# A hybrid decoder block on eight cores: interleaved query tiles, stationary P^T, resident MLP weights, and the normalisation of x from a host-transposed copy

## Chip, cores, metric

The kernel runs on all 8 NeuronCores of one Trainium2 chip. The metric is the device time of the slowest core in microseconds. A program on all cores has a fast state and a slow one, in which the cores of a die show a lower clock and take longer. The ratios below are of fast runs alone, and the profiles shown are of fast runs; a time in us given for a run is the median of all its executions.

Engine names in the profile: PE is the matrix engine (PEld its weight loads, which overlap it), ACT the activation engine, DVE the vector engine, POOL and SP the two that issue DMA (transfers between DRAM and on-chip memory) here. PSUM is the memory that PE writes its results to. The granted clock is the share of PE's full clock that the throttle let through. POOL issues the loads that cast fp32 to bf16, SP all others. L386 means line 386 of that kernel's source.

## The reference

Four sequences of 4096 tokens, width 1024. Cut to what matters:

```python
xn = rmsnorm(x, norm_mix_g)                      # per token
u = xn @ w_in                                    # 5120 columns: conv b,c,v | q,k,v | two gates
y_a = short_gated_conv(b_g, c_g, v_a, conv_w) @ w_a_out
s = q k^T / 8 - slope_h * (i - j), causal        # 4 heads, two softmax maps each
o = (softmax(s0) - lam * softmax(s1)) @ v        # then rmsnorm over the head's 128 values
x = x + (g_a * y_a + g_b * (o @ w_b_out)) @ w_o
x = x + relu(rmsnorm(x) @ w_mlp_in)**2 @ w_mlp_out
return rmsnorm(x) * norm_final_g
```

Two cores share a sequence. Each computes K and V for all 4096 tokens and the rest for 2048 queries of its own.

## The kernel before

Every engine has its own in-order instruction list; a recorder turns buffer reads and writes into semaphores. The parts that matter (cuts marked `# ...`):

```python
# phase 1: a token tile is squared, scaled, and transposed by PE
S.op("act", ... activation(xb, xt, AF.Square, accum_out=st[:, 0:1]) ...)
S.op("act", ... Ln ...); S.op("act", ... Exp, scale=-0.5 ...)        # rstd, per partition = per token
S.op("dve", ... tensor_scalar_mul(xb, xt, st[:, 2:3]) ...)
for c in range(8):
    S.op("pe", ... transpose(pst[:, c, :], xb[:, c*128:(c+1)*128], ident) ...)
S.op("dve", ... tensor_tensor(dst, pst, gcols, ALU.mult) ...)        # x normalised and transposed
# ...
# phase 2: a step = 128 keys x 512 queries x 2 maps
def emit_pv(n):        # V stationary, P^T moving
    mm(Ops[:, m, cs:512], Vt[:, kt, h*128:(h+1)*128], PT[:, m, cs:512], ...)
def emit_lsum(n):      # row sums: ones stationary, P^T moving
    mm(Lps[:, m, cs:512], ones_bf, PT[:, m, cs:512], ...)
# per head: copy O and L, 128x1024 reciprocal, multiply, subtract, norm
# ...
S.barrier()            # between projections, attention, gates, MLP
# phase 4: eight groups of 512 hidden columns, W1 and W2 streamed, x_mid accumulated by DVE
```

The softmax here doesn't subtract the row's maximum and nothing guards it: scores larger than these inputs give would overflow.

## Time and profile before

| run | us |
|---|---|
| fast runs of the first four | 1544.24, 1546.27 |
| slow runs of the first four | 1663.52, 1740.64 |

The page of the profiled run gives busy time per engine, and PE's busy share and granted clock in 40 equal slices (9 is 90% or more):

```profile
span 1546.6 us, 22141 instructions; the slowest of 8 cores (1531.8 to 1546.6 us)
...
PE 1376.5 (89%) x6824; PEld 584.5 (38%) x6824; DVE 709.2 (46%) x963; ACT 712.6 (46%) x1066; POOL 67.5 (4%) x72
...
PE   1989999878999999999367888897999999999995
...
PEclk9999999989999999999788999999999999999998
```

PE is nearly full apart from the first slice, the change from attention to gates (slices 20 and 21) and the gates, where it is busy 255 of 321 us. The table by windows says the same by stage. Its columns are: window and length, busy us of each engine with instructions in brackets, granted clock, DMA share, GB/s. The rows are projections, attention, gates and merge, MLP, last norms.

```profile
0.00:291.00 291.00, 244.32 (x1352) 118.44 (x1352) 134.20 (x231) 94.97 (x210) 5.29 (x13) 0.99 0.37 84
291.00:760.00 469.00, 431.35 (x2176) 149.91 (x2176) 197.45 (x111) 347.48 (x350) 2.38 (x3) 0.96 0.06 10
760.00:1081.00 321.00, 255.22 (x1250) 115.91 (x1248) 136.91 (x213) 160.16 (x306) 29.73 (x34) 0.91 0.54 86
1081.00:1507.00 426.00, 425.38 (x1959) 192.30 (x1960) 214.07 (x364) 81.24 (x140) 11.32 (x14) 0.99 0.22 36
1507.00:1546.60 39.60, 20.28 (x91) 7.90 (x88) 26.56 (x45) 28.70 (x60) 18.78 (x8) 0.84 0.53 212
```

One step of attention in the timeline (start, length, engine, what):

```profile
601.13 1.04 PE L348 MATMUL ps_all<-big 128*128 128x512 bf16 x4
601.30 1.11 ACT L675 ACTIVATE big<-ps_all,big 128x1024 bf16<-128x1024 f32 x1 [0.18 <-PE ps_all L350]
602.10 0.39 PE L350 MATMUL ps_all<-big 64*128 64x512 bf16 x2
602.42 1.04 PE L348 MATMUL ps_all<-big 128*128 128x512 bf16 x4
```

From one group of four to the next it is 602.42 - 601.13 = 1.29 us, of which the exponential takes 1.11. PE binds, and ACT is close.

### The profile page before, as it was taken

The numbers are of one execution on the slowest core, as the hardware profiler recorded it, in microseconds if no ns is written. First come the engines' busy times: TensorE is split into PE (matmuls) and PEld (weight loads), VectorE is DVE, ScalarE is ACT, GpSimd is POOL, SyncE is SP. The second block draws the span as 40 slices with busy tenths as digits, with TensorE's granted clock in tenths as the row PEclk, the third lists the DMA queues.
The fourth block names the chain that finished last, engine by engine and source line by source line (L and its number), as shares of the span: only waits on it lengthen the run. The fifth ranks groups of instructions, "written<-read, shape, count | busy, mean of one in ns | idle before, by whom it ended". The sixth has DMA issues, their size and how long they took to land.

```text
span 1546.6 us, 22141 instructions; the slowest of 8 cores (1531.8 to 1546.6 us)
## 1 busy us (share of the span) xinstructions
PE 1376.5 (89%) x6824; PEld 584.5 (38%) x6824; DVE 709.2 (46%) x963; ACT 712.6 (46%) x1066; POOL 67.5 (4%) x72
## 2 busy tenths in 40 slices
PE   1989999878999999999367888897999999999995
PEld 0444444323333333333123434343444444444441
DVE  2444454476553332333323454455253563564476
ACT  2553322356778878888244555463312112102217
POOL 0000000000000000000000000000000000000004
PEclk9999999989999999999788999999999999999998
DMA  8861100330000000000197254443331313121105
GB/s 163 182 159 53 44 28 1 54 56 1 1 1 1 1 1 1 1 0 1 19 259 103 36 74 53 57 56 55 53 57 31 53 29 55 28 32 25 28 11 208
DMA packets 63907, 80.06 MB, mean 52 GB/s; under 512 B 2984, under 2 KB 48168, under 8 KB 63792
## 3 DMA queue, kind: packets, MB, share of 16 engines
q0 software_dynamic: 53120, 44.04, 20.2%
q1 hardware_dynamic: 10672, 34.60, 7.0%
q8 instruction: 58, 0.95, 0.2%
q14 instruction: 57, 0.47, 0.1%
HBM read 114.29 MB, written 8.39 MB: 79 GB/s over the span
## 4 chain that ended last, share of the span: by engine, by line
PE 77%; DVE 8%; DMA 5%; ACT 5%; issue 3%; SPq 0%; POOL 0%; POOLq 0%; DVEq 0%; ACTq 0%
PE ps_all L348 70%; PE ps_all L350 6%; DMA big<-w_in 3%; DMA big<-xs 2%; DVE big L706 2%; DVE big L700 1%; DVE big L809 1%; ACT big L675 1%; ACT big L962 1%; ACT big L790 1%; PE ps_all L387 1%; PE ps_all L807 1%; ACT big L973 1%; DVE big L856 0%; DVE big L390 0%
## 5 line engine op out<-in xcount | busy, mean ns | idle before, releaser
L348 PE MATMUL ps_all<-big 128*128 128x512 bf16 (+3 forms) x5600 | 1270.6, 378 | 98.9 <-ACT big L834 24.4
L348 PEld LDWEIGHTS ps_all<-big 128*128 128x128 bf16 x5600 | 517.4, 100 | 741.2 <-issue 212.1
L675 ACT ACTIVATE big<-ps_all,big 128x1024 bf16<-128x1024 f32 (+1 forms) x320 | 329.1, 1049 | 101.2 <-PE ps_all L350 68.0
L997 ACT ACTIVATE big<-ps_all 128x512 bf16<-128x512 f32 x128 | 76.4, 597 | 319.1 <-PE ps_all L348 319.1
L1011 DVE TENSOR_TENSOR big<-ps_all,big 128x512 f32<-128x512 f32 x256 | 175.7, 690 | 39.3 <-PE ps_all L348 36.1
L350 PE MATMUL ps_all<-big 64*128 64x512 bf16 (+3 forms) x736 | 130.0, 350 | 11.6 <-ACT big L675 6.9
L998 DVE TENSOR_TENSOR big<-big 128x512 bf16<-128x512 bf16 x128 | 54.4, 425 | 175.9 <-ACT big L997 175.9
L706 DVE RECIPROCAL big<-big 128x1024 f32<-128x1024 f32 x16 | 104.8, 6552 | 2.0 <-DVE big L705 0.5
L700 DVE COPY big<-ps_all 128x1024 f32<-128x1024 f32 x16 | 19.6, 1222 | 175.5 <-PE ps_all L348 175.5
L350 PEld LDWEIGHTS ps_all<-big 64*128 64x128 bf16 x736 | 36.1, 93 | 147.6 <-issue 141.3
L850 DVE TENSOR_TENSOR big<-ps_all,big 128x512 f32<-128x512 f32 x32 | 22.1, 691 | 143.7 <-PE ps_all L348 94.1
L790 ACT ACTIVATE big<-big 128x1024 bf16<-128x1024 f32 x28 | 29.6, 1056 | 96.9 <-DVE big L789 91.3
L366 ACT ACTIVATE big<-big 128x1024 bf16<-128x1024 f32 (+1 forms) x33 | 34.9, 1058 | 56.9 <-DVE big L488 26.2
L319 POOL DMA_DIRECT2D big<-w_in x34 | 29.9, 883 | 710.3 <-DVE big L725 469.3
L387 PE MATMUL ps_all<-big 128*128 128x128 bf16 (+1 forms) x264 | 21.5, 228 | 39.4 <-DVE big L365 31.0
L376 DVE TENSOR_SCALAR big<-big 128x1024 bf16<-128x1024 f32 (+1 forms) x33 | 25.0, 759 | 53.1 <-ACT big L370 53.1
L390 DVE TENSOR_TENSOR big<-ps_all,big 128x1024 bf16<-128x1024 bf16 (+1 forms) x33 | 39.1, 1186 | 3.4 <-PE ps_all L387 3.3
L705 DVE COPY big<-ps_all 128x1024 f32<-128x1024 f32 x16 | 19.6, 1224 | 41.5 <-PE ps_all L348 41.4
L401 DVE CAST big<-ps_all 128x512 bf16<-128x512 f32 x24 | 16.5, 688 | 43.0 <-PE ps_all L348 43.0
L387 PEld LDWEIGHTS ps_all<-big 128*128 128x128 bf16 (+1 forms) x264 | 18.2, 102 | 47.1 <-issue 40.9
L725 DVE SCALAR_TENSOR_TENSOR big<-big 128x512 bf16<-128x512 f32 x16 | 12.0, 750 | 50.5 <-ACT big L724 50.5
L834 ACT ACTIVATE big<-ps_all,big 128x512 f32<-128x512 f32 x32 | 21.7, 679 | 27.3 <-PE ps_all L348 27.3
(67 smaller groups left out, 558.9 us busy)
## 6 DMA issues: line engine op xcount, KB each, us to landing
big<-xs SPq DMA_DIRECT2D x48, 512.0 KB, 7.8
big<-w_in POOLq DMA_DIRECT2D x32, 512.0 KB, 6.8
big<-w POOLq DMA_DIRECT2D x16, 1024.0 KB, 8.7
out<-big SPq DMA_DIRECT2D x16, 512.0 KB, 2.9
big<-w_in POOLq DMA_DIRECT2D x4, 1024.0 KB, 33.3
big<-w_in POOLq DMA_DIRECT2D x1, 2048.0 KB, 25.0
big<-w_o POOLq DMA_DIRECT2D x1, 2048.0 KB, 29.0
big<-w_a POOLq DMA_DIRECT2D x1, 1024.0 KB, 12.1
```

The lines of the kernel that those rows point to most:

```text
L348: S.op("pe", lambda e: e.matmul(out, lhsT, rhs, start=start, stop=stop), reads=reads, writes=writes)
L350: S.op("pe", lambda e: e.matmul(out, lhsT, rhs, start=start, stop=stop, tile_position=tp), reads=reads, writes=writes)
L366: S.op("act", lambda e: e.activation(xb[:ntok], xt[:ntok], AF.Square, accum_out=st[:ntok, 0:1]), reads=[xkey, skey], writes=[xbkey, skey])
L387: S.op("pe", lambda e, c=c: e.transpose(pst[:, c, :ntok], xb[:ntok, c * 128:(c + 1) * 128], ident[:ntok, :ntok]), reads=[xbkey, "ident"], ...
L390: S.op("dve", lambda e: e.tensor_tensor(dst, pst[:, :, :ntok], gcols.unsqueeze(2).to_broadcast([128, 8, ntok]), ALU.mult), reads=[pkey, gk ...
L675: S.op("act", lambda e: e.activation(PT[:, :, cs:512], Sps[:, buf, :, cs:512], AF.Exp, bias=btab[:, bidx:bidx + 1], scale=0.125), reads=[" ...
L700: S.op("dve", lambda e: e.tensor_copy(c["Ocp"], Ops), reads=["O"], writes=[c["k"] + "O"])
L706: S.op("dve", lambda e: e.reciprocal(c["Lcp"], c["Lcp"]), reads=[k + "L"], writes=[k + "L"])
L790: S.op("act", lambda e: e.activation(xb, xt, AF.Square, accum_out=st[:, 0:1]), reads=[xkey, skey], writes=[xbkey, skey])
L997: S.op("act", lambda e, r=r, ph=ph: e.activation(r, ph, AF.Relu), reads=[phk], writes=[rk])
L998: S.op("dve", lambda e, r=r, fc=fc, sl=sl: e.tensor_tensor(hb[:, fc, sl * 512:(sl + 1) * 512], r, r, ALU.mult), reads=[rk], writes=["h2_%d ...
L1011: S.op("dve", lambda e, T=T, half=half, pz=pz: e.tensor_tensor(x_mid[:, T, half * 512:(half + 1) * 512], pz, x_mid[:, T, half * 512:(half ...
```

## The change

The intent: halve PE's work for PV by making P^T the stationary operand, with V and a column of ones moving, so the row sum comes along; give each core every second 128-query tile, so that causal trimming acts on both halves of the keys; have the host hand over x transposed, so that PE transposes no norms; keep MLP weights resident and accumulate over all 4096 hidden columns in PSUM; remove barriers. The source has a mode that interleaves projections with attention; in this version it is off. A rewrite, so only its core is shown (cuts marked `...`):

```diff
-    mm(Ops[:, m, cs:512], Vt[:, kt, h*128:(h+1)*128], PT[:, m, cs:512], ...)
-    mm(Lps[:, m, cs:512], ones_bf, PT[:, m, cs:512], ...)
+    mm(oview(m, t), PT.ap[:, m, t*128:(t+1)*128], v.ap[:, h, 0:129], start, ..., skip=True)
...
-    # Square, Ln, Exp, scale, 8 PE transposes, multiply by g       (per 128 tokens)
+    def xT_load(blk, pieces=2):                    # x^T from the host, cast by POOL's DMA
+        wload(XT[s], xT_d[blk], q * n, n, 512)
+    def load_tok(blk, t):                          # the same tokens again, for the statistics
+        ld(xt.ap, xs_d[r0:r0 + 128, :], [xt])      # two buffers, SP
+    def row_bcast(blk, src, dst, n, p):            # rstd: one per partition -> one per column
+        row = rr_sp[blk, 0:n]                      # a DRAM scratch row
+        S.dma("sp", ... dma_start(out=row.rearrange("(t p) -> p t", p=128), in_=src.ap[:, 0:4]))
+        ld(dst.ap, rr_sp[blk:blk+1, 0:n].partition_broadcast(128), [dst], [key])
+    def nrm(c):                                    # x^T * g * R, by DVE, 8 of them
+    steps = [a, sq(0), sq(1), sq(2), sq(3), r, b, nrm(0), nrm(2), nrm(4), nrm(6)]   # + spill of xn
...
+    W += spread(conv(1) + kv(6), prelude(2))       # a block's prelude runs in the block before it
+    plan = PLAN if merge else [(n_a0, 0), (n_a1, 0), (n_a2, 0), (n_a3, 0)]          # merge=False
...
+    m_w1()                                         # W1 (8 x 2 MB fp32) and a quarter of W2: POOL
+    until(10 ** 9 if False else sum(1 for k, _ in W if k))    # last conv, gates, merge
+    for q in (1, 2, 3): cload(W2[q]...)
+    m_load(0)                                      # MLP input back from its spill: SP
```

Block 4, the first, needs no row: its rstd is applied to the exponent's scale and to V, where it is per partition.

## The prediction

> Times are fast-state (before: 1544 us; I take its runs of 1664 and 1741 for slow).
>
> **What bounds it now.** Page: PE busy 1376 of 1547 us; chain of waits 77% PE. By windows:
> - 0-281 us, projections: first matmul group at 38 us, then PE nearly full.
> - 295-760, attention: a full step (128 keys x 512 queries x 2 maps) takes 1.29 us (timeline): four 128x512 matmuls 0.86, the QK pair with array-mode switches 0.43. The exponential takes 1.11, so PE binds, ACT close behind. The first four heads take 17 us each behind a DVE chain with a 6.55 us reciprocal.
> - 760-1081, gates: PE busy 254 of 321; idle for weight DMA (767-820) and the norm chain (Square, scale, transpose, L809).
> - 1081-1507, MLP: PE 100%, 215 ns per matmul.
> - 1507-1547: final norms.
>
> **Unchanged:** about 4096 dense matmuls x 215 ns = 882 us.
>
> **What the change does.**
> 1. PV and row sums: P^T stationary, V plus a ones column moving; the build has 2176 matmuls of 129 columns for 1280 mostly 512 wide. Warm 128-wide transposes cost 56 ns each here (16 in 1.06 us, 8 in 0.61): 122 us for about 260. The Trainium skill ("TensorE: Matmul & The Clock Gate", Back-to-back issue gap) gives 81 ns sustained at N=128; this trace shows 56.
> 2. Attention becomes ACT-bound. 384 exponentials (168 of 1024, 152 of 512, 24 of 768, 40 of 256) at before's 1.11/0.69/0.90/0.48 us = 332 us, like before's 329: finer trimming is spent on splitting head 0 in two. Back to back, ACT instructions overlap by 0.09 us: 300 to 332. Add group 0 (DVE epilogue about 9 us per head), small pairs, and 6 us PE idle per flush: 360 to 390 against 465. PE idles 30% of it; nothing is interleaved.
> 3. Host-supplied x^T and folded scales remove norm transposes and stalls; reloads of spilled tiles return about 5 us per gate group, transposes 2 us.
> 4. The POOL queue is in order: W1 and a quarter of W2 (20 MB fp32) go ahead of the last gate weights and Wo (6 MB). Cast loads took 20.2% of 16 engines' span for 44 MB bf16: about 285 GB/s of fp32 (estimate). So Wo lands 90 us after attention 3, where PE could start z at 62: stall about 30 us. The conv weights queue behind attention 0's last POOL op: 13 us stall. At the start 14 MB precede the second K/V block: attention 0 starts near 73 us.
> 5. MLP 442 us plus 5-8 for reloading its input; tail 10 us for 39.
>
> **Sum.** Start 73; attention 45+70+105+139; projections between 69+57+57; last conv 21; gates 4x57+36+28 = 292; MLP 450; tail 10: about 1390. I say 1400, range 1335 to 1505 (high end: slow runs in a median). Faster 0.93, same 0.04, slower 0.03.
>
> **Right if** ACT is over 85% busy in attention groups 2 and 3, about 2.1 us per full pair; PV costs 56-60 ns; PE has a 15-35 us gap in gate group 0 ended by a w_g or w_o DMA; MLP matmuls stay at 215 ns; the tail is under 15 us.
>
> **Wrong if** PV costs 80 ns or more (+40 us); cast loads run below 250 GB/s (start and gate group 0, +30); flush and small-pair bubbles are twice mine; or denser matmuls draw a lower granted clock. Faster if large contiguous weight rows load well above 300 GB/s.

## The result

1799.18 us median of four (1785.01 to 1846.02); the two fast runs are 1799.94 and 1785.01. A ratio here is the mean time of one kernel's fast runs over that of the other's in the same rounds, so it isn't quite the ratio of the medians quoted. It is 1.1595, with a 95% interval of 1.1511 to 1.1679: the changed kernel is 16% slower.

The page after, the lines that answer to those above:

```profile
span 1798.4 us, 20663 instructions; the slowest of 8 cores (1776.2 to 1798.4 us)
...
PE 1267.2 (70%) x7168; PEld 611.5 (34%) x7168; DVE 501.3 (28%) x1135; ACT 529.0 (29%) x744; POOL 61.6 (3%) x97
...
PE   4055528266555759667772788797709999999998
...
PEclk9576669687777888677986678898959999999999
```

PE is busy 109 us less and idle for 531 us. The holes are in the first half. In the clock row, 9s appear mostly where PE is full. This trace holds two reduced clocks: 0.50 for 532 us of the core shown, against 120 us on the core shown of the kernel before, and 0.81 for 236 us between 682 and 1096 us. The 0.81 is seen on the four cores of die 0 only (104 to 243 us); die 1 has none and took 1781 us (median of its cores) against 1794, so it is worth some 13 us (an estimate from that difference). The windows below run from the first to the last exponential of each attention group, so odd rows are projections and even rows attention; then come last conv, gates and merge in one row, MLP, tail.

```profile
0.00:136.00 136.00, 44.91 (x162) 16.98 (x162) 23.67 (x49) 15.16 (x26) 12.75 (x25) 0.75 0.59 107
136.00:188.00 52.00, 29.93 (x230) 18.66 (x230) 29.71 (x109) 25.59 (x36) 3.02 (x3) 0.62 0.02 6
188.00:344.00 156.00, 67.31 (x335) 29.13 (x334) 43.64 (x92) 17.40 (x35) 8.53 (x13) 0.70 0.43 78
344.00:427.00 83.00, 54.91 (x547) 35.52 (x546) 28.88 (x107) 59.77 (x74) 3.02 (x3) 0.84 0.02 6
427.00:545.00 118.00, 64.38 (x271) 26.93 (x270) 39.45 (x81) 14.77 (x28) 5.25 (x7) 0.74 0.37 73
545.00:665.00 120.00, 84.18 (x870) 54.75 (x868) 31.04 (x111) 95.02 (x114) 3.02 (x3) 0.86 0.01 4
665.00:762.00 97.00, 72.51 (x268) 28.63 (x267) 38.59 (x78) 8.77 (x17) 5.46 (x9) 0.74 0.36 77
762.00:918.00 156.00, 116.44 (x1188) 75.24 (x1188) 26.93 (x104) 131.07 (x156) 3.42 (x4) 0.84 0.12 23
918.00:1346.00 428.00, 288.64 (x1259) 124.87 (x1256) 139.23 (x218) 66.95 (x105) 8.43 (x15) 0.79 0.50 120
1346.00:1790.00 444.00, 443.50 (x2047) 200.75 (x2048) 97.92 (x189) 93.33 (x158) 8.15 (x15) 1.00 0.13 46
1790.00:1798.40 8.40, 0.51 (x3) 0.01 (x1) 2.19 (x3) 1.15 (x2) 0.54 (x1) 0.74 0.15 62
```

| stretch | predicted | measured |
|---|---|---|
| projections, the four | 73+69+57+57 = 256 | 136+156+118+97 = 507 |
| attention, the four | 359 | 52+83+120+156 = 411 |
| last conv, gates, merge | 21+292 = 313 | 428, entry of the MLP included |
| MLP and tail | 460 | 452 |

The projections hold 251 us of the error. One of them, 427 to 545 us, in the chain of waits (start, length, what it stood on):

```profile
467.17 19.31 DMA rr_sp<-big
486.55 5.94 DMA big<-rr_sp
...
501.55 8.02 DMA big<-xs
...
512.18 4.37 DMA big<-xs
...
519.38 16.29 DMA rr_sp<-big
535.74 6.28 DMA big<-rr_sp
```

Twice in this stretch a row of 512 rstd values is written to DRAM (19.31 and 16.29 us) and read back over 128 partitions (5.94 and 6.28); the tokens for the second block's statistics are loaded only after the first block is normalised. PE is busy 64 us of the 118. The write also keeps the list of SP waiting: over the whole kernel SP stood 110.1 us, in eight waits, until such a write had landed, before it could issue the read and the loads behind it. The list of DMA issues (count, KB each, median us to landing) has both transfers:

```profile
rr_sp<-big SPq DMA_DIRECT2D x7, 2.0 KB, 16.3
big<-rr_sp SPq DMA_DIRECT2D x7, 256.0 KB, 6.3
```

Attention itself went as meant. A pair of key tiles in its steady part:

```profile
859.85 6.24 ACT L670 ACTIVATE big<-ps_all,big 128x1024 bf16<-128x1024 f32 x6
860.10 1.73 PE L386 MATMUL ps_all<-big 64*128 64x512 bf16 x20 [0.37 <-ACT big L670]
860.42 1.11 PEld L386 LDWEIGHTS ps_all<-big 128*128 128x128 bf16 x18 [0.23 <-issue]
862.11 1.73 PE L386 MATMUL ps_all<-big 64*128 64x512 bf16 x20 [0.29 <-ACT big L670]
```

A pair (two steps of the kernel before, 2.58 us there) takes 2.01 to 2.1 us (2.19 where the clock is 0.81), ACT runs without a gap, six exponentials in 6.24 us, and PE is idle 0.3 to 0.4 us of each pair. The Trainium skill ("ScalarE: Activation LUTs", What ACT_TABLE_LOAD costs) says that back-to-back ACTIVATEs overlap by about 93 ns; here six that take 1.11 us each alone (in the kernel before) take 6.24 in a row, 84 ns less at each of the five joints, which nearly agrees.

At the change from one head to the next it looks different (the second line is the window 850 to 855 us, columns as above):

```profile
849.33 4.84 PE L386 MATMUL ps_all<-big 128*128 128x129 bf16 x36 [3.63 <-DVE big L706]
850.00:855.00 5.00, 4.68 (x37) 3.20 (x36) 2.27 (x13) 2.21 (x2) 1.01 (x1) 0.50 0.02 5
```

PE waits 3.63 us, and then 36 matmuls take 4.84 us at a clock of 0.50, where 40 take 3.46 in the steady part. In the four attention stretches ACT is busy 311 of 411 us: it stands still 100 us, 6.2 us for each of the sixteen heads.

Two long PE waits follow later, at the first gate group and at the MLP (idle time before the group and its releaser in brackets):

```profile
981.00 3.57 PE L386 MATMUL ps_all<-big 128*128 128x512 bf16 x8 [27.55 <-DMA big<-xn_sp]
1001.86 56.21 PE L386 MATMUL ps_all<-big 128*128 128x512 bf16 x208 [17.29 <-DMA big<-ya_sp]
...
1346.50 3.93 PE L386 MATMUL ps_all<-big 128*128 128x512 bf16 x9 [47.61 <-DMA big<-x_sp]
```

### The profile page after: what moved, and what is told of

Its sections match the earlier page's. It is cut to its first block, busy times and chain, and to the rows that moved or that the text cites. A ratio compares the mean times of both kernels' runs of the same rounds, so it can differ in the third digit from the quotient of the medians.

```text
span 1798.4 us, 20663 instructions; the slowest of 8 cores (1776.2 to 1798.4 us)
## 1 busy us (share of the span) xinstructions
PE 1267.2 (70%) x7168; PEld 611.5 (34%) x7168; DVE 501.3 (28%) x1135; ACT 529.0 (29%) x744; POOL 61.6 (3%) x97
## 4 chain that ended last, share of the span: by engine, by line
PE 52%; DMA 24%; DVE 10%; ACT 7%; issue 4%; POOL 1%; DVEq 0%; SPq 0%; ACTq 0%; POOLq 0%
PE ps_all L386 51%; DMA big<-xs 7%; ACT big L670 6%; DMA rr_sp<-big 6%; DMA big<-ya_sp 3%; DMA big<-rr_sp 3%; DMA big<-x_sp 2%; DVE big L489 1%; DMA x_sp<-big 1%; DVE big L706 1%; DVE big L710 1%; DVE big L720 1%; POOL big L715 1%; ACT big L430 1%; DMA xm_sp<-big 1%
## 5 line engine op out<-in xcount | busy, mean ns | idle before, releaser
L386 PEld LDWEIGHTS ps_all<-big 128*128 128x128 bf16 (+1 forms) x6976 | 598.5, 103 | 1103.6 <-issue 700.4
L670 ACT ACTIVATE big<-ps_all,big 128x1024 bf16<-128x1024 f32 (+3 forms) x384 | 315.5, 882 | 240.1 <-PE ps_all L386 226.0
L780 ACT ACTIVATE big<-ps_all,big 128x512 f32<-128x512 f32 x64 | 44.0, 687 | 209.5 <-PE ps_all L386 209.5
L791 DVE SCALAR_TENSOR_TENSOR big<-big,ps_all 128x512 f32<-128x512 f32 x64 | 44.0, 688 | 178.3 <-PE ps_all L386 178.3
L489 DVE SCALAR_TENSOR_TENSOR big<-big 128x512 bf16<-128x512 bf16 x56 | 39.1, 744 | 166.6 <-DMA big<-rr_sp 166.6
L430 ACT ACTIVATE big<-big 128x1024 bf16<-128x1024 f32 x32 | 33.9, 1058 | 172.4 <-DMA big<-xs 172.0
L675 DVE TENSOR_TENSOR big<-big 128x256 bf16<-128x256 bf16 x64 | 18.7, 292 | 223.5 <-ACT big L670 223.5
L915 ACT ACTIVATE big<-big 128x1024 bf16<-128x1024 f32 x16 | 16.9, 1056 | 208.3 <-DVE big L910 208.3
L910 DVE SCALAR_TENSOR_TENSOR big<-ps_all,big 128x512 f32<-128x512 f32 x32 | 24.0, 751 | 163.2 <-PE ps_all L386 163.2
L818 ACT ACTIVATE big<-big 128x1024 bf16<-128x1024 f32 x16 | 16.9, 1057 | 74.0 <-DVE big L814 74.0
L727 PE MATMUL ps_all<-big 128*128 128x128 bf16 x64 | 8.1, 268 | 42.0 <-DVE big L720 42.0
L814 DVE SCALAR_TENSOR_TENSOR big<-ps_all,big 128x512 f32<-128x512 f32 x32 | 22.0, 689 | 34.9 <-PE ps_all L386 21.0
L828 PE MATMUL ps_all<-big 128*128 128x128 bf16 x128 | 11.5, 242 | 22.4 <-DVE big L817 22.3
L830 DVE TENSOR_TENSOR big<-ps_all,big 128x1024 bf16<-128x1024 bf16 x16 | 19.6, 1224 | 22.4 <-DMA x_sp<-big 20.7
```

Source lines behind the costliest of these rows:

```text
L386: S.op("pe", lambda e: e.matmul(out, lhsT, rhs, start=start, stop=stop, skip_group_check=skip), reads, writes)
L430: act(lambda e: e.activation(junk.ap, xt.ap, AF.Square, accum_out=ss1[blk].ap[:, t:t + 1]), [xt], [junk, ss1[blk]])
L489: dve(lambda e, k=k: e.scalar_tensor_tensor(x[k].ap, x[k].ap, ccol(C_GMIX + k), R_b.ap, ALU.mult, ALU.mult), [x[k], cst, R_b], [x[k]])
L670: act(lambda e, a=a, b=b, c=c, s=s, PT=PT, scale=scale: e.activation(PT.ap[:, :, a:b], Sb[s][:, :, a:b], AF.Exp, bias=ccol(C_BTAB + c), sc ...
L780: act(lambda e: e.activation(t.ap, ps, AF.Tanh, bias=hbg.ap[:, 8 * w + dm:8 * w + dm + 1], scale=0.5), [key, hbg], [t])
L791: dve(lambda e: e.scalar_tensor_tensor(t.ap, t.ap, 1.0, ps, ALU.add, ALU.mult), [key, t], [t])
```

## The experiments

Sixteen runs, three rounds each (five for the last); the kernel before had medians of 1544.2, 1547.42, 1548.49 and 1550.47 us. Gains in us are taken from the 1799 above. It includes two slow runs; the two fast ones are 15 us apart with a mean of 1792.5, and by fast runs alone most gains are some 5 to 8 us smaller. Theory A: the DRAM round trip of the rstd row, on a serial chain per block, holds the projections. Rivals: the denser matmuls draw a lower clock (B); the bytes of x, which are read twice (C); the separate stretches themselves; the in-order POOL queue.

### 1. No round trip, wrong values (e1_copy)

```diff
-        S.dma("sp", w, [src], [key])
-        ld(dst.ap, rr_sp[...].partition_broadcast(128), [dst], [key])
+        dve(lambda e: e.tensor_copy(dst.ap[:, 0:n], src.ap[:, 0:1].to_broadcast([128, n])), [src], [dst])
```

> The DRAM round trip of the rstd row is replaced by an on-chip copy with the same dependency (wrong values on purpose; same input bytes, same statistics). In the changed kernel the row write took 8 to 20 us to land and the broadcast read 5 to 16, seven times in series. Theory A (the round trip sits on a serial chain that bounds the projection stretches): the four stretches 0-146, 195-340, 437-572, 672-800 us (554 together, 330 to 360 of it idle or cold PE) fall to about 350 in sum, total 1560 to 1620, and the mean granted clock rises from 0.84 to 0.90 or more. Theory B (the denser matmuls draw a lower clock): the clock stays near 0.84, total within 3% of 1799. Theory C (the stretches are bound by the bytes of x, read twice): bytes are the same, so the total moves under 3%.

1614.2 us, 1.0445 of before (1.0421 to 1.0468), relative error 0.041 as intended. The four projection stretches:

```profile
0.00:84.00 84.00, 43.25 (x162) 16.64 (x162) 23.96 (x51) 15.16 (x26) 12.84 (x25) 0.86 0.77 166
137.00:234.00 97.00, 64.64 (x330) 28.48 (x328) 40.23 (x88) 15.63 (x31) 8.53 (x13) 0.84 0.54 119
320.00:390.00 70.00, 60.34 (x275) 26.55 (x273) 39.12 (x82) 13.86 (x26) 5.25 (x7) 0.93 0.49 115
511.00:580.00 69.00, 58.31 (x268) 25.84 (x266) 38.75 (x79) 8.97 (x17) 5.53 (x9) 0.93 0.43 97
```

They sum to 320 us in place of 507 (the expectation's 554 had wider edges), a gain of 187 us, which is the gain of the whole kernel (1799 - 1614 = 185; 178 by fast runs). The input bytes are the same, so C falls as the main cause. The mean granted clock went from 0.84 to 0.89 (0.90 was expected) and in these stretches from 0.70-0.75 to 0.84-0.93 without any matmul being changed, so most of the low clock followed from the idle PE; B falls as the main cause. The 0.81 on die 0 is absent from this run's trace, so it adds some 13 us to the comparison at most. The Trainium skill ("TensorE: Matmul & The Clock Gate", Part 1) describes a clock that rises with activity and falls back when PE idles, which agrees: 0.50 was granted for 351 to 371 us of each core here, and for 524 to 563 us in the changed kernel.

### 2. The same row in 16-byte runs, right values (e2_rows)

```diff
-        r0 = blk * 512 + t * 128
-        ld(xt.ap, xs_d[r0:r0 + 128, :], [xt])
+        rows = xs_d[blk * 512:(blk + 1) * 512, :].rearrange("(p t) d -> p t d", t=4)
+        ld(xt.ap, rows[:, t, :], [xt])
...
-        out=row.rearrange("(t p) -> p t", p=128)
+        out=row.rearrange("(p t) -> p t", t=4)
```

> Right values; the statistics tile holds tokens 4p+t, so the row is written as 128 runs of 16 bytes in place of 512 runs of 4 bytes. If the number of tiny writes makes the write slow, its landing falls from a median of 16 us to 5 or less and the total by about 60 to 90 us. If it is queueing behind the large loads or the receipt of a DRAM write, it stays over 10 us and the total within 2%.

1695.05 us, correct, 1.0928 of before (1.0903 to 1.0953): 104 us gained, more than the 60 to 90 expected, by choosing which tokens share a partition. The list of DMA issues:

```profile
rr_sp<-big SPq DMA_DIRECT2D x7, 2.0 KB, 2.5
big<-rr_sp SPq DMA_DIRECT2D x7, 256.0 KB, 4.4
```

The write fell from 16.3 to 2.5 us with the same 2 KB and the same loads around it, so it was the 512 runs of 4 bytes, not the writing to DRAM as such, that made it slow. The Trainium skill ("DMA: Bandwidth & Descriptors", Rules for kernel authors) says that a last dimension that isn't contiguous becomes one descriptor per element. This agrees: from the changed kernel (first line) to this run (second) the packets fall by 2688, which is 7 x (512 - 128).

```profile
DMA packets 38021, 119.57 MB, mean 66 GB/s; under 512 B 7680, under 2 KB 12160, under 8 KB 34464
DMA packets 35333, 119.57 MB, mean 71 GB/s; under 512 B 4992, under 2 KB 9472, under 8 KB 31776
```

The number of runs isn't all: the row for the convolution's halo (the tokens just before each query tile, 32 values) still goes as 4-byte runs in this kernel, and took 10.4 us in a stretch (186 to 200 us) in which the DMA engines were full.

### 3. Statistics one block earlier, round trip kept (e3_ahead)

```diff
-    R_b = ar.take("R", [512], F32)
+    R_r = [ar.take("R%d" % k, [512], F32) for k in range(3)]
...
-    W += spread(kvq(0), prelude(5))
+    W += spread(kvq(0), prelude(5, 1) + prelude_halo())     # normalise 5, statistics of 1
```

> Right values; the round trip is kept, but each block's statistics start one block earlier, with three row buffers, and the halo moves before attention 0. Theory A with the chain only exposed by lack of lookahead: PE waits for the normalised tiles shrink to under 100 us in sum, total 1560 to 1650, while the write still takes 10 us or more to land. If the loads of x (token-major) through two buffers and the in-order SP queue bind instead, the chain just shifts and the total falls by less than 60 us.

1711.02 us, correct, 1.1072 (1.1054 to 1.1091): 88 us gained, less than the 150 or more that was expected. The stretches became 163, 92, 88 and 68 us: the last three shrank by 123 us, and the start grew by 27, because two blocks' statistics now stand ahead of the first attention. The write still took 14.4 us. So in the later stretches much of the chain was exposed for want of lookahead; at the start there is nothing to hide it under.

### 4. Order of the weight bursts (e5_loads)

```diff
-    m_w1()
-    until(all chunks)
+    until(n_w1)          # after 16 chunks of gate group 0
+    m_w1()
+    until(n_g2 + 32)
+    m_load(0)            # MLP input back, during gate group 2
+    until(all chunks)
```

> Only DMA order in the gate and MLP stretches changes: the 20 MB burst of W1 and W2 starts after the 16th chunk of gate group 0, and the first MLP input tile is loaded back during gate group 2. Theory: the reload of the spilled tiles was starved by weight bursts on the same 16 DMA engines; then the 43 us gap at 959-1002 falls to 8 to 12, the 30 us gap ahead of the MLP to under 5, total 1730 to 1745 (3 to 4% less). Rival: the gaps are the latency of spill and reload itself; then they stay over 25 us each. Projections and attention are unchanged.

1738.71 us, correct, 1.1266 (1.1234 to 1.1298): 60 us less, in the expected range, but only in part for the expected reason. PE's waits at gate group 0 and ahead of the MLP (us in total, times, longest):

```profile
PE ps_all L386 <- DMA big<-xn_sp: 31.1, 1, 31.1
PE ps_all L386 <- DVE big L837: 3.5, 1, 3.5
```

The wait ahead of the MLP fell from 47.6 to 3.5 us. The waits in gate group 0 stayed (31.1 and 12.1 us against 27.6 and 17.3), because later in the program isn't later in time: POOL has nothing to wait for and runs ahead, and issued the burst at 934.28 us, before SP issued the reload at 937.94. By fast runs alone the gain is 53 us: 44 from the MLP's entry, and 8 from a projection start that was earlier in this run, which the edit doesn't explain.

### 5. Merged stretches, round trip kept (e4_merge)

```diff
-def build_program(merge=False):
+def build_program(merge=True):
```

> Right values; only the argument merge is turned on: the projections of the next group (and conv, gates after group 3) are issued between attention pairs by the kernel's own plan, everything else as changed, round trip included. If the separate stretches are the loss (theory: PE idles in attention about 40%, and the norm chain only runs outside it), the chain and its DRAM round trip hide under attention: total 1350 to 1500. Rival: the in-order queues carry the waits of the norm chain into attention (the Square on ACT and the row write on SP stand in the same queues as the exponentials and stores), so most of it stays exposed: total 1600 or more.

1744.81 us, correct, 1.1283 (1.1253 to 1.1313). Letting projections run between attention pairs is worth 54 us, not 300: the rival holds. The row writes are 8% of this run's chain of waits; the chain's Squares and DMA issues stand in the same in-order queues as the exponentials and the stores of attention. That its waits are carried along in them is a reading of the program, not shown; what the list of waits shows is that ACT still stood 137.6 us for the token loads ahead of the Squares (172.0 in the changed kernel).

### 6. Broadcast on PE, right values (e7_pebcast), and together with the loads (x_sep)

```diff
-        S.dma("sp", w, [src], [key])
-        ld(dst.ap, rr_sp[...].partition_broadcast(128), [dst], [key])
+        for t in range((n + 127) // 128):      # diagonal of rstd
+            dve(... tensor_scalar_mul(dgb.ap[:p, t*m:(t+1)*m], ident[:p, 0:m], src.ap[:p, t:t+1]) ...)
+        mm(ps[:, 0:n], ones_f.ap[:p, :], dgb.ap[:p, 0:n], True, True, ...)     # fp32
+        dve(... tensor_copy(dst.ap[:, 0:n], ps[:, 0:n]) ...)
```

> Right values; the row is broadcast on chip: diagonal of rstd times a matrix of ones in fp32 on PE (one 128x512 fp32 matmul per block, 0.63 us in the kernel before), no DRAM round trip. Theory A, as confirmed by the wrong-valued copy (1614): 1605 to 1650. If the copy was fast only because its values were degenerate or the halo was taken from elsewhere: over 1700.

1667.83 us, correct, 1.0774 (1.0751 to 1.0797): 131 us gained, 18 us above the range. The projection stretches take 106, 116, 88 and 79 us, 389 in sum against 320 with the wrong-valued copy. The matmul stands in PE's queue, and PE waits there 92.1 us for what DVE prepares for it (L456, the diagonal).

> The on-chip broadcast together with the reordered weight and MLP-input loads: two independent stretches, so the gains add: 1799 less about 180 less about 60, 1540 to 1590. If they overlap (for instance the DMA freed in one is taken in the other) it stays over 1600.

1619.77 us, correct, 1.0475 (1.0454 to 1.0495). 179 us gained against 131 + 60 = 191 measured singly: the gains nearly add. My range missed because it took the wrong-valued copy's 180 for the broadcast's 131.

### 7. Attention's 52 us over the prediction (e8_ocopy, e9_late, e6_order)

At a head's end PE waits about 3.6 us for the epilogue's last read of the PSUM output before it may start the next head. Copy the output out at once:

```diff
+            for b_, lo, n_ in ((4, 0, 390), (5, 390, 390), (6, 780, 260)):
+                dve(... tensor_copy(o_cp.ap[:, lo:lo + n_], bank(b_)[:, 0:n_]) ...)
```

> At each head's end the three PSUM banks of the attention output are copied to SBUF at once (about 1.5 us) and the epilogue works on the copy; before it the next head's first PV waits 3.6 to 4 us for the epilogue's reads. If that wait is the attention stretches' loss over the exponentials' 303 us, 15 to 40 us of the 412 us go away (total down 1 to 2%). If the short last pairs and their mask latency are the loss, under 10 us.

1822.51 us, correct, 1.1789 (1.1753 to 1.1825): slower than the changed kernel. The waits of PE on the epilogue's transposes (L732 there, L727 in the changed kernel) doubled. So the transposes two slots later as well:

```diff
-            deferred.append((2, d1)); deferred.append((4, d2))
+            deferred.append((3, d1)); deferred.append((6, d2))
```

> The changed kernel with the attention outputs copied out at once as in the earlier run (1822) and, in addition, the transposes of the epilogue two slots later (6 in place of 4). There PE waited 86 us for the transposes' input (43 before), so the wait had only moved. If that is why the copy did not help, attention falls by 15 to 40 us against 412, total 1760 to 1790. If not, it stays at 1800 to 1825.

1816.66 us, correct, 1.1743 (1.1691 to 1.1796): a miss. The list of who waited for whom (total us, times, longest), in the changed kernel, in e8_ocopy and in e9_late:

```profile
PE ps_all L727 <- DVE big L720: 42.0, 16, 8.6
PE ps_all L732 <- DVE big L725: 86.0, 16, 10.3
PE ps_all L732 <- DVE big L725: 65.6, 13, 10.9
```

The copy-out took the wait from the PSUM reads (43.9 us on the epilogue's last read, in the changed kernel) to the transposes, and placing these later shortened it by 20 us, but attention stayed at 53, 85, 121 and 156 us.

The rival for the 52 us was the three short diagonal pairs at each head's end:

```diff
-            js = [4*g] + list(range(4*g)) + [4*g+1, 4*g+2, 4*g+3]
+            js = [4*g, 4*g+1, 4*g+2, 4*g+3] + list(range(4*g))
```

> On the changed kernel: the three short diagonal pairs of each head come second to fourth in place of last. If the short pairs' latency (mask, small exponentials) is attention's loss over the exponentials' 303 us, attentions 1 to 3 (84, 120, 156 us) each lose 4 to 10 us. If the head change (epilogue reads and transposes in PE's queue) is the loss, they stay within 3 us or grow.

1828.8 us, correct, 1.1776 (1.1754 to 1.1797). Attentions 1 to 3 took 90, 126 and 161 us, 5 to 7 more than before. The order of the short pairs isn't the loss; the head change is what is left, by elimination. Whether its cost is the chain of small DVE operations or the clock of 0.50 after the wait, no run separates: with the copy-out PE's wait before the first PV is 1.01 us in place of 3.63, but the 33 matmuls after it still take 3.86 to 4.38 us, and the wait returns before the transposes (4.3 to 4.8).

### 8. What still holds the projections (e10_onetile, e11_recip)

Both on the kernel with the broadcast on PE (1667.83), with wrong values.

```diff
-            st[1] = load_tok(blk, 1)      # and tiles 2, 3 later
+            st[1] = st[2] = st[3] = st[0]
```

> On the kernel with the on-chip broadcast (1668): each block's statistics squared four times from one loaded tile in place of four tiles (wrong values on purpose; 1.5 MB less per block read token-major through two buffers). If those loads are what still holds the projections (ACT waited for them 145 us in the lookahead version), the total falls by 50 to 90 us. If the loads of x^T and of weights hold them, by less than 25.

1634.9 us, 1.0537 (1.0518 to 1.0556): 33 us less, between the two expectations. Reading x a second time costs this much here, mostly at the start (106 to 86 us) and after attention 0 (116 to 102).

```diff
-        S.op("pool", ... tensor_tensor(..., m05..., ALU.pow), ...)      # three places
+        S.op("dve", ... reciprocal(...), ...)
```

> On the kernel with the on-chip broadcast (1668): the power -1/2 on POOL is replaced by a reciprocal on DVE (wrong values on purpose), so POOL only issues loads and can prefetch weights and x^T during attention. If the in-order POOL queue delays those loads, the gap after attention 0 (116 us) shrinks by 20 to 40 and the total by 30 to 60. If not, within 15 us.

1663.68 us, 1.0731 (1.0716 to 1.0746): 4 us. The gap after attention 0 did shrink, from 116 to 101 us, but the start grew from 106 to 113 and the next gap from 88 to 92. So the order of POOL's queue is not what holds the projections in sum.

### 9. Towards a faster version (v_merge7, v_sep, v_merge, v_merge2)

v_merge7 is merge=True with the broadcast on PE.

> Merged stretches (as in the merge run, 1745) with the on-chip broadcast of rstd (as in 1668). If merging failed because the DRAM round trip's waits were carried into attention, removing it lets the merge hide the projections: 1400 to 1500. If the loads of x token-major and the Squares in ACT's queue are the carried wait, 1580 to 1640 (the two single gains, 55 and 132, at most added).

1614.0 us median (1602.3 to 1683.5), correct; two of the four runs are slow. The two fast ones are 1602.3 and 1614.35, 58 us under the fast runs of e7_pebcast; with the round trip merging gave 48 by fast runs. So the two gains add, and the round trip was not what kept merging small.

v_sep keeps the stretches apart and combines broadcast, lookahead, the copy-out of e9_late, and a real dependency for the bursts:

```diff
-            cload(W1[g]..., [W1[g]])
+            cload(W1[g]..., [W1[g]], [g_xn] + g_on + g_ya)     # wait for the reloads
...
-    cload(W2[q]..., [W2[q]])
+    cload(W2[q]..., [W2[q]], ["x2sp3_3"])                      # wait for the last spill
```

> Separate stretches; on-chip broadcast, statistics one block ahead, weight bursts held until the spilled tiles are back (by a dependency this time: in the earlier run the POOL queue had simply run ahead), attention outputs copied out at once with the transposes two slots later. Expected against 1620 of the earlier combination: lookahead 60 to 100 less in the projection gaps (101, 116, 88, 78 there), gate stall 25 to 30 less, last store before the MLP 15 less, attention 10 to 30 less: 1430 to 1510.

1600.45 us, correct, 1.035 (1.031 to 1.0391): 20 us less than x_sep where 110 to 190 were expected. The wait at gate group 0 fell to 20.5 us, but a 22.7 us wait turned up at a transpose later in that group, under the burst that now comes later. The projection stretches were 103, 91, 82 and 87 us, 20 us less in sum than x_sep's 101, 116, 88 and 78.

v_merge is merge=True with broadcast, lookahead and held-back bursts.

> Merged, with the on-chip broadcast, statistics one block ahead, and weight bursts held back. If PE is then the only bound, its busy floor of 1140 to 1220 plus start, gate reloads and tail gives 1330 to 1430, under the kernel before's 1545. If ACT's in-order queue (exponentials behind Squares that wait for loads) binds, over 1500.

1557.47 us, correct, 1.0034 (0.999 to 1.0079): not told apart from the kernel before (the record has it as unclear), and a miss by over 120 us of the 1330 to 1430 expected if PE alone had bound; over 1500 was expected if ACT's in-order list bound, which no run isolates. v_merge2 also issues the W1 burst after gate group 2's reloads and the MLP's first input later:

```diff
-            cload(W1[g]..., [W1[g]], [g_xn])
+            cload(W1[g]..., [W1[g]], [g_xn] + g_on + g_ya)
...
-    m_w1()
-    m_load(0)
+    until(n_g2 + 8)
+    m_w1()
+    until(n_g2 + 32)
+    m_load(0)
```

> The merged version (1557, 1547 in its profile) with the W1 burst held until gate group 2's spilled tiles are back and the MLP's first input loaded later; there 923 to 992 us was spent on four loads under the burst. Expected 1490 to 1520, 2 to 4% under the kernel before. If the wait returns at the next loads, over 1535.

1543.47 us median of five, correct, 0.9956 (0.9943 to 0.997). It is 0.4% under the kernel before, clear of noise but short of the 1490 to 1520 expected.

```profile
span 1541.9 us, 20446 instructions; the slowest of 8 cores (1528.8 to 1541.9 us)
...
PE 1220.6 (79%) x7074; PEld 583.4 (38%) x7184; DVE 513.2 (33%) x1172; ACT 529.9 (34%) x744; POOL 62.5 (4%) x98
```

PE is still idle 321 us. About 53 of them are in the first 104 us, before the first exponential.

## Why the prediction was wrong, point by point

- **Step 3, "Host-supplied x^T and folded scales remove norm transposes and stalls"**: this failed, and it is the main error. It counted what the new normalisation removes and priced nothing for how rstd gets from partitions to columns. That path, through a DRAM row in 4-byte runs, took 16.3 + 6.3 us (medians) seven times, on a chain that starts again only when the block before is done. The projection stretches took 507 us where the prediction had 256; removing the round trip alone took them to 320 (shown by e1_copy), and writing the same row in longer runs took 104 us off the total with right values (e2_rows). What is left over the prediction, 64 us, is in part the second reading of x (33 us in e10_onetile, which stands on another kernel) and otherwise open.
- **Step 4, the stalls of loads**: the sizes of the queues were right, but not what PE would wait for. Wo landed at 1022 us, 104 us after attention 3 where 90 were predicted, yet no stall of PE was seen on w_g, w_o or the conv weights. The stall in gate group 0 (27.6 + 17.3 us against 28 predicted) was ended by the reloads of x-normed and conv outputs from SP, which share the DMA engines with the 20 MB from POOL. The Trainium skill ("DMA: Bandwidth & Descriptors", Issuing engines are not separate DMA queues) says just that; the conv reload, which the chain of waits charges with 42.55 us under the burst, took 4.8 to 7.3 us there in later groups. Holding the burst back by a dependency (v_sep) left 20.5 us of the first wait and none of the second, 24 of the 45 us less, but a wait of 22.7 us turned up later in the group. That the first of the two waits is close to the 28 predicted is luck.
- **Step 5, "plus 5-8 for reloading its input"**: 47.6 us, under the burst of W2; loading it earlier brought it to 3.5 (e5_loads). The MLP itself was right, 444 us with 217 ns a matmul, and so was the tail (8 us).
- **Step 2, attention**: ACT-bound with 2.0 to 2.1 us a pair, as predicted. The sum was 411 against 359, and ACT's share in groups 2 and 3 was 95/120 = 79% and 131/156 = 84%, just under the 85% named. What the prediction had too small is the loss between heads: ACT stood still 100 us, 6.2 us for each head. Three tries did not reduce it.
- **Step 1, PV**: right. Eighteen weight loads, 16 of them PV's, took 1.11 us, 62 ns each, and in the steady part PE kept ahead of ACT. The skill's sustained 81 ns at N=128 ("TensorE: Matmul & The Clock Gate", Back-to-back issue gap) is longer than what this trace shows.
- **"Denser matmuls draw a lower granted clock"**, named as a risk: not shown. The mean clock was lower (0.84), mostly through 0.50 after idle stretches. In the steady part of the denser attention it was 1.00 (865 to 880 us). The 0.81 that die 0 shows for part of attention 3 (780 to 800 us), the last projections and the gates is absent from die 1 of the same execution, which ran the same matmuls, and from all but three of the sixteen experiments' traces (e9_late, v_sep, v_merge). What brings it on stays open.

The differences add up by stage: 251 (projections) + 52 (attention) + 115 (gates and MLP entry) - 8 = 410 us, which is 1798 - 1388.

Also named as part of the loss at first, and not shown so: the separate stretches. Merging was worth 48 us with the round trip and 58 without, by fast runs.

## What to carry to other kernels

When a change replaces a compute chain by data movement, price each new transfer by its number of contiguous runs and by what must happen before the next one can start, not by its bytes; then look for the one serial chain per block and compare its length with the compute that is there to hide it. A rearranged tile assignment (which token sits in which partition) turned 512 runs of 4 bytes into 128 of 16 here, at no cost that the runs show. Moving a DMA later in the program didn't move it past the reloads in time here, as its queue had nothing to wait for; a dependency did.

## What the Trainium skill lacked or had wrong

- "DMA: Bandwidth & Descriptors" has no time for small transfers in very short runs: a 2 KB write to DRAM as 512 runs of 4 bytes took 7.9 to 19.9 us (median 16.3), as 128 runs of 16 bytes 1.4 to 7.6 (median 2.5), with bulk loads in flight in both.
- "TensorE: Matmul & The Clock Gate", Part 1, tells to budget 13/16 of the clock for dense matmuls on three or more cores of a die. In fast runs the MLP, with all eight cores busy, shows a granted clock of 0.99 to 1.00 and 217 ns per 512-column matmul. The figure itself does occur: 0.81 for 104 to 243 us on the cores of one die in the changed kernel's trace, outside its MLP.
- The same page, Back-to-back issue gap, gives 81 ns sustained at N=128; here 62 ns per weight load in the 129-column stream, and 1.73 us for a whole pair of 16 such matmuls and four QK matmuls.
